# Down-projection weights of a gated FFN: gain and Strassen sums prepared in the up-projections and kept in DRAM, residual rows added to straight from PSUM

## The chip, the cores and the metric

The kernel runs on one core of a Trainium2 chip. The metric is device time in microseconds (us) of one execution; lower is better. A core has TensorE (PE, the matmuls, with PEld for its weight loads), VectorE (DVE), ScalarE (ACT), GpSimd (POOL), and SyncE (SP), whose queue issues nearly all DMAs here. Data lies in DRAM, in SBUF (128 partitions) and in PSUM, where matmuls write.

## The reference

One step of a layer: token mixing with three recurrences, then a gated FFN, then a norm. The change concerns the last product of the FFN and the residual. In the reference `T` is 2048 for the prompt and 4 for each of 8 samples, `D_MODEL` 1024, `D_FF` 2816; all in float32:

```
h = _rmsnorm(x, p['norm_ffn'][l]) * (1 + sc2) + sh2
gate, b_ffn = _causal_dwconv(h @ p['ffn_w_gate'][l], b_ffn, p['ffn_conv_w'][l])
gate = gate + p['ffn_conv_b'][l]
x = x + g2 * ((jax.nn.silu(gate) * (h @ p['ffn_w_up'][l])) @ p['ffn_w_down'][l])
...
y = _rmsnorm(x, final_norm)
```

`g2` is a vector of 1024 gains for a sequence, so for the prompt `g2 * (a @ w)` equals `a @ (w * g2)` with each column of `w` taken times its gain.

## The kernel before

Float32 accuracy comes from splitting: `split` (L1812) makes of a tile a rounded part hi (ACT, L1813) and the rest lo (DVE, L1814), and `s_prod` (L1816) makes each block product of three matmuls, hi·hi, hi·lo and lo·hi (L1822 to L1824). On top of it the FFN's products use the Strassen-Winograd scheme: of a 2x2 arrangement of blocks seven products, 1 to 7, take the place of eight, at the price of sums of blocks. The sums of the stationary side are made by `s_combo` on POOL (L1790 to L1802), four for each set of seven products. The sums of the moving side are made once for many sets. A set of eight plain products stands where the sums of the moving side are not ready.

The up-projections (`ffn_up_s`, here from about 1845 to 2299.5 us) run over sets of products with weights as the stationary side; each product is 24 matmuls of 264 columns. DVE there splits the weights (`w_lo<-w_raw,w_hi`), joins the products' partial sums (L2029, L2030) and applies a causal convolution (L1997); the gated rows go to DRAM as `aT`.

The down-projection (`ffn_down_s`, 2299.5 to 2838.4 us) has its moving side, w_down, in three thirds of 3, 4 and 4 row-blocks (`KH`). Inside a third it runs over 8 sets of 256 tokens: the first set plain (products named C.. when complete), the others by Strassen. A generator, `down_tiles`, prepares the third to come: it starts two sets before the old third ends and goes on into the first sets of the new one, because a tile's room is free only when the old third's last product with that tile is done (`freed`). It loads four quarters of w_down for each row-block, splits them as tiles 1, 2, 3 and B, then loads quarters again, makes 5, 6 and 7 by `t_sums` (one subtraction on POOL, L1807, two on DVE, L1808 and L1809) and 4 by two subtractions on POOL (L2213), and splits those. While it has quarters in hand it also issues the matmuls of the 32 sample tokens (`d_sample`, L2239, `mm_ds`, 176 passes in all).

After a product, `after` joins the results. Products 1, 5 and 6 are copied out of PSUM by ACT (`snap`, L2299, into `d_y`). When the partner is done, DVE adds it from PSUM (L2347), multiplies by the gains g2 (L2348), and one step later POOL adds the residual row x (L2351; in the last set DVE does). Plain products and 4 need one multiplication from PSUM (L2344) and the same POOL addition. The row is then stored, or normed and written out in the last third. Residual rows x are loaded three products ahead into the ring of raw tiles (tag "wr", 8 buffers), which the w_down loads share; partial sums have a ring of their own, "sn", of 8.

The order on each engine is not that of the Python code: a list scheduler arranges the instructions by estimated times, and each engine then runs its list in order. DMAs stand in SP's list and wait there for what they store and for a free buffer.

Of the kernel before, what the change touches and what calls it, by code (L numbers as in the profile page):

```python
# [73 lines left out]
class Kern:  # L74
# [94 lines left out]
    def setup(self):  # L169
# [33 lines left out]
        sc("sdn", [NS, D])  # L203

# [1709 lines left out]
    def ffn_up_s(self, pts, open1, down):  # L1914
# [215 lines left out]
        more, at = more(), [0]  # L2130
        for n, (s, P, U, t, b, first, done) in enumerate(seq):
# [15 lines left out]
        self.flush()  # L2147

# [7 lines left out]
    def down_tiles(self, pts, n, freed):  # L2156


        nc = self.nc
        w = self.i["ffn_w_down"][0].rearrange("(k p) c -> p k c", p=128)  # L2160
        kh, k0 = KH[n], 2 * sum(KH[:n])

        T = self.dT[n] = {P: [None] * kh for P in "1234567B"}

        def load(q, k):
            i, j = int(q[0]) - 1, int(q[1]) - 1
            r = self.w_raw()[:, :512]
            self.ld(r, w[:, k0 + kh * i + k, 512 * j:512 * j + 512])
            return r

        def put_t(P, k, raw):
            tag = P.replace("B", "4")
            p = pts[k // 2](tag)
            T[P][k] = t = (p.tile([128, 2 * NP], F32R, name="t_hi", tag=f"{tag}h{k % 2}")[:, :512],
                           p.tile([128, 2 * NP], F32R, name="t_lo", tag=f"{tag}l{k % 2}")[:, :512])
            self.split(*t, raw)

        raws = {}
        order = [(q, P, k) for q, P in (("11", "1"), ("21", "2"), ("22", "3"), ("12", "B")) for k in range(kh)]
        for x in order[:SWR - 1]:  # L2180
            raws[x] = load(x[0], x[2])
        for m, x in enumerate(order):
            while x[1].replace("B", "4") not in freed:
                yield
            put_t(x[1], x[2], raws.pop(x))
            if m + SWR - 1 < len(order):
                y = order[m + SWR - 1]
                raws[y] = load(y[0], y[2])
            if m % 2:
                yield  # L2190


        while not {"5", "6", "7"} <= freed:
            yield
        q = None
        for k in range(kh + 1):
            old, q = q, None
            if k < kh:
                q = {x: load(x, k) for x in ("12", "11", "22")}
                yield  # L2200
                self.d_sample(k0 + k, (q["11"], q["12"]))
                self.t_sums(q)
            for P in "576" if old else ():
                put_t(P, k - 1, old[P])
                yield
        while "C" not in freed:
            yield
        r = [(load("21", k), load("22", k)) for k in range(2)]
        for k in range(kh):
            yield  # L2210
            self.d_sample(k0 + kh + k, r[k])
            for x in T["6"][k]:
                nc.gpsimd.tensor_tensor(r[k][0], r[k][0], x.bitcast(F32), op=ALU.subtract)  # L2213
            if k:
                put_t("4", k - 1, r[k - 1][0])
            if k + 2 < kh:
                r.append((load("21", k + 2), load("22", k + 2)))
        yield
        put_t("4", kh - 1, r[kh - 1][0])

    def ffn_down_s(self, p, pts, work, freed):
# [9 lines left out]
        g = p.tile([128, D], F32, name="g2")  # L2231
        self.ld(g, self.ap(self.dram["modr"], 5 * D, [[0, 128], [1, D]]))
# [9 lines left out]
        self.d_sample = sample  # L2242
# [30 lines left out]
        outs, xs = {}, {}  # L2273
# [463 lines left out]
```

## Time and profile before

| | us |
|---|---|
| median of 3 runs | 2845.62 (2843.83 to 2852.76) |
| profiled execution | 2848.95 |
| its span in the trace | 2847.2 |

The page's head and its slices of the span:

```profile
span 2847.2 us, 54532 instructions
PE 2715.1 (95%) x19969; PEld 2462.4 (86%) x19969; DVE 1888.8 (66%) x3767; ACT 1267.9 (45%) x2795; POOL 930.2 (33%) x1353
PE   6999999999999999999999999989999989999888
DVE  4535777577676778565565546596776677867777
POOL 3311223311113422111121102254344447565675
```

A slice is 71 us; each digit is the busy share in tenths. The up-projections by Strassen are the slices from about 26 to 32, the down-projection the last eight: there POOL, little used before, is busy for half and more of the time. Busy time of PE is counted from the start of the first to the end of the last of the matmuls that follow one another without a gap, so that a lower clock shows as longer matmuls and not as idle time; the prediction therefore counts matmuls and takes their undisturbed step.

### The profile page before, as it was taken

Reading aid. Unit: us, or ns where it says so; the run is one execution under the profiler, and the core shown is the slowest. Engines: PE = TensorE matmul, PEld = TensorE weight load, DVE = VectorE, ACT = ScalarE, POOL = GpSimd, SP = SyncE. Lnnn points to the kernel's source line nnn. Section 1 sums busy time; section 2 is a strip of 40 time slices with the busy share of each in tenths; the row PEclk is TensorE's granted clock in tenths of the full one; section 3 lists DMA queues with packets and bytes.
Section 4 is the critical chain, followed back from the end, with each engine's and each line's share of the span. In section 5 each row is a group of like instructions: output and inputs, shape, how many; then the busy total and the mean of one; then the engine's idle time right before and its main releaser. Section 6 shows DMA issues by size and latency. Waiting matters only on the chain.

```text
span 2847.2 us, 54532 instructions
## 1 busy us (share of the span) xinstructions
PE 2715.1 (95%) x19969; PEld 2462.4 (86%) x19969; DVE 1888.8 (66%) x3767; ACT 1267.9 (45%) x2795; POOL 930.2 (33%) x1353
## 2 busy tenths in 40 slices
PE   6999999999999999999999999989999989999888
PEld 4999888889989999999999989989999967667566
DVE  4535777577676778565565546596776677867777
ACT  4534445455554545544443323454444443423333
POOL 3311223311113422111121102254344447565675
PEclk8999999999999999999999999999999999999999
DMA  6465436675556697553553345752222266756542
GB/s 234 132 207 151 127 111 175 182 227 144 176 165 196 213 283 198 159 154 114 183 151 105 107 147 153 217 180 80 90 69 79 77 198 188 255 157 194 177 147 96
DMA packets 543106, 455.30 MB, mean 160 GB/s; under 512 B 83302, under 2 KB 475142, under 8 KB 541814
## 3 DMA queue, kind: packets, MB, share of 16 engines
q1 hardware_dynamic: 542838, 451.82, 52.4%
q8 instruction: 157, 2.57, 0.4%
q14 instruction: 111, 0.91, 0.1%
HBM read 310.17 MB, written 141.53 MB: 159 GB/s over the span
## 4 chain that ended last, share of the span: by engine, by line
PE 44%; DVE 6%; POOL 5%; DMA 4%; issue 3%; ACT 1%; SPq 0%; POOLq 0%; DVEq 0%; ACTq 0%
PE mm_f L608 5%; PE mm_f L610 5%; PE mm_f L609 5%; PE s_x L1823 3%; PE s_x L1822 3%; PE s_x L1824 3%; PE d_ps L1822 3%; PE d_ps L1823 3%; PE d_ps L1824 2%; POOL d_y L2351 2%; PE s_y L1822 1%; PE s_y L1823 1%; PE s_y L1824 1%; DVE t_lo L1814 1%; DVE w_lo L1814 1%
## 5 line engine op out<-in xcount | busy, mean ns | idle before, releaser
L608 PE MATMUL mm_f<-g_hi,w_hi 128*128 128x384 f32 (+2 forms) x2016 | 663.0, 329 | 4.0 <-ACT g_hi L579 3.9
L609 PE MATMUL mm_f<-g_lo,w_hi 128*128 128x384 f32 (+2 forms) x2016 | 652.8, 324 | 0.5 <-DVE g_lo L580 0.4
L610 PE MATMUL mm_f<-g_hi,w_lo 128*128 128x384 f32 (+2 forms) x2016 | 652.4, 324 | 0.0
L608 PEld LDWEIGHTS mm_f<-g_hi,w_hi 128*128 128x128 f32 x2016 | 381.9, 189 | 25.9 <-issue 14.8
L609 PEld LDWEIGHTS mm_f<-g_lo,w_hi 128*128 128x128 f32 x2016 | 382.6, 190 | 6.8 <-issue 4.8
L610 PEld LDWEIGHTS mm_f<-g_hi,w_lo 128*128 128x128 f32 x2016 | 382.2, 190 | 6.4 <-issue 5.7
L1822 PE MATMUL d_ps<-t_hi,w_hi 128*128 128x512 f32 x627 | 257.5, 412 | 23.0 <-ACT t_hi L1813 12.8
L1823 PE MATMUL d_ps<-t_lo,w_hi 128*128 128x512 f32 x627 | 256.2, 409 | 13.4 <-DVE t_lo L1814 13.4
L1824 PE MATMUL d_ps<-t_hi,w_lo 128*128 128x512 f32 x627 | 248.0, 405 | 6.3 <-DVE w_lo L1814 6.3
L556 DVE TENSOR_TENSOR w_lo<-w_raw,w_hi 128x512 fp32r<-128x512 f32 (+1 forms) x236 | 163.7, 700 | 75.8 <-ACT w_hi L555 71.6
L555 ACT CAST w_hi<-w_raw 128x512 fp32r<-128x512 f32 (+1 forms) x236 | 144.1, 619 | 137.7 <-PE mm_f L609 96.2
L1822 PE MATMUL s_x<-t_hi,w_hi 128*128 128x264 f32 x704 | 200.7, 285 | 2.5 <-DVE sy L2030 1.4
L1823 PE MATMUL s_x<-t_lo,w_hi 128*128 128x264 f32 x704 | 200.4, 285 | 0.0
L1824 PE MATMUL s_x<-t_hi,w_lo 128*128 128x264 f32 x704 | 199.1, 283 | 0.5 <-DVE w_lo L1814 0.5
L1814 DVE TENSOR_TENSOR w_lo<-a_raw,w_hi 128x512 fp32r<-128x512 f32 (+1 forms) x159 | 154.8, 984 | 52.0 <-ACT w_hi L1813 49.0
L2351 POOL TENSOR_TENSOR d_y<-d_y,t_raw 128x512 f32<-128x512 f32 x92 | 144.8, 1576 | 127.3 <-DVE d_y L2348 53.8
L1813 ACT CAST w_hi<-a_raw 128x512 fp32r<-128x512 f32 (+1 forms) x159 | 91.6, 583 | 208.7 <-PE d_ps L1823 125.8
L1822 PEld LDWEIGHTS d_ps<-t_hi,w_hi 128*128 128x128 f32 x627 | 121.6, 194 | 68.6 <-ACT t_hi L1813 16.7
L1814 DVE TENSOR_TENSOR w_lo<-w_raw,w_hi 128x512 fp32r<-128x512 f32 x156 | 112.9, 726 | 76.7 <-ACT w_hi L1813 75.2
L1823 PEld LDWEIGHTS d_ps<-t_lo,w_hi 128*128 128x128 f32 x627 | 121.5, 194 | 48.5 <-DVE t_lo L1814 19.3
L1813 ACT CAST w_hi<-w_raw 128x512 fp32r<-128x512 f32 x156 | 96.2, 619 | 138.0 <-PE s_x L1823 69.6
L1824 PEld LDWEIGHTS d_ps<-t_hi,w_lo 128*128 128x128 f32 x627 | 121.6, 194 | 36.7 <-DVE w_lo L1814 8.1
(574 smaller groups left out, 6811.1 us busy)
## 6 DMA issues: line engine op xcount, KB each, us to landing
t_raw<-in_ffn_w_down_dram SPq DMA_DIRECT2D x99, 256.0 KB
w_raw<-in_w_in_dram SPq DMA_DIRECT2D x96, 256.0 KB
t_raw<-x SPq DMA_DIRECT2D x96, 256.0 KB
w_raw<-in_ffn_w_gate_dram SPq DMA_DIRECT2D x94, 256.0 KB
w_raw<-in_ffn_w_up_dram SPq DMA_DIRECT2D x94, 256.0 KB
ada_w<-in_w_ada_dram SPq DMA_DIRECT2D x32, 512.0 KB
R<-recB SPq DMA_DIRECT2D x16, 1024.0 KB
x<-d_y SPq DMA_DIRECT2D x64, 256.0 KB
```

Of the source, the lines that this page charges most:

```text
L555: nc.scalar.copy(hi[:, :n], raw[:, :n])
L556: nc.vector.tensor_sub(lo[:, :n], raw[:, :n], hi[:, :n].bitcast(F32))
L608: nc.tensor.matmul(ps[:, :N], wh, hi[:, k, :N], start=(k == 0), stop=False)
L609: nc.tensor.matmul(ps[:, :N], wh, lo[:, k, :N], start=False, stop=False)
L610: nc.tensor.matmul(ps[:, :N], wl, hi[:, k, :N], start=False, stop=(k == 7))
L1813: self.nc.scalar.copy(hi, src)
L1814: self.nc.vector.tensor_sub(lo, src, hi.bitcast(F32))
L1822: self.nc.tensor.matmul(ps, hi[:, k], th, start=(start and k == 0), **f)
L1823: self.nc.tensor.matmul(ps, hi[:, k], tl, start=False, **f)
L1824: self.nc.tensor.matmul(ps, lo[:, k], th, start=False, stop=(k == n - 1), skip_group_check=True)
L2351: (nc.vector if s == len(sets) - 1 else nc.gpsimd).tensor_tensor(y, y, x, op=ALU.add)
```

## The change

1. `down_sums`, new, runs in the up-projections, advanced once a product from step `8 * n_plain + 8` on. For each of the 11 row-blocks it loads the four quarters of w_down (128x512, 256 KB), has DVE multiply each by its gains, stores the results (tiles 1, B, 3, 2) to a new scratch tensor `wdT` in DRAM, has POOL make four subtractions (5, 7, 6, 4), and stores these. That is 44 loads, 44 multiplications, 44 subtractions and 88 stores. The gains g2 are loaded there.
2. `down_tiles` loads finished tiles from `wdT` and splits them, in the order 1, 5, 6, 2, 3, B, 7, 4. The sums of L1807 to L1809 and L2213 are gone, the number of splits is the same.
3. `after` adds products straight from PSUM to the residual row on DVE: products 1, 5 and 6 to the rows 11, 22 and 12, then the partners, or for plain products and 4 the one result. The copies by ACT, the multiplications by gains and the separate additions on POOL are gone. The residual rows are now loaded into the ring "sn", of 10 buffers, three products ahead of the first addition.
4. The sample's matmuls are a generator of their own, `samples`, with 44 loads of w_down, advanced in the list `states` after products 1, 3 and 6 of sets that are not a third's last.

The loads from w_down so go from 99 to 88, and 88 loads from and 88 stores to `wdT` are new.

```diff
+NSN = 10
...
+            if n >= 8 * n_plain + 8:
+                next(sums, None)
...
+    def down_sums(self):
...
+        g = self.pev.tile([128, D], F32, name="g2", tag="g2", bufs=1)
+        self.ld(g, self.ap(self.dram["modr"], 5 * D, [[0, 128], [1, D]]))
...
+                for _ in range(2):
+                    yield
+                for x, P in (("11", "1"), ("12", "B"), ("22", "3"), ("21", "2")):
+                    j = int(x[1]) - 1
+                    nc.vector.tensor_tensor(q[x], q[x], g[:, 512 * j:512 * j + 512], op=ALU.mult)
+                    put(P, x)
+                    if x in ("12", "21"):
+                        yield
+                yield
+                for P, o, a, b in (("5", "11", "12", "11"), ("7", "12", "22", "12"), ("6", "22", "22", "11"),
+                                   ("4", "21", "21", "22")):
+                    nc.gpsimd.tensor_tensor(q[o], q[a], q[b], op=ALU.subtract)
+                    yield
+                    put(P, o)
...
     def down_tiles(self, pts, n, freed):
...
+        order = [(P, k) for P in "15623B74" for k in range(kh)]
...
+            self.ld(r, self.dram["wdT"]["123B567".index(P) if P != "4" else 7, row + k])
...
-                self.t_sums(q)
...
-            for x in T["6"][k]:
-                nc.gpsimd.tensor_tensor(r[k][0], r[k][0], x.bitcast(F32), op=ALU.subtract)
...
-                xs[outs[m]] = x = self.w_raw()[:, :512]
-                self.ld(x, place(*outs[m]))
+                xs[needs[m]] = x = p.tile([128, 512], F32, name="d_y", tag="sn", bufs=NSN)
+                self.ld(x, place(*needs[m]))
...
-            if P in "156":
-                c["s" + P] = snap(c["V" if P == "5" else "X"])
+            add = lambda name, ps: nc.vector.tensor_tensor(xs[s, name], ps, xs[s, name], op=ALU.add)
+            first = {"1": ("11", "X"), "5": ("22", "V"), "6": ("12", "X")}.get(P)
+            if first:
+                add(first[0], c[first[1]])
...
-                nc.vector.tensor_tensor(y, c[{"1": "Y", "3": "V", "7": "X"}[P]], y, op=ALU.add)
-                nc.vector.tensor_tensor(y, y, g[:, cs], op=ALU.mult)
-
-            def rest():
-                (nc.vector if s == len(sets) - 1 else nc.gpsimd).tensor_tensor(y, y, x, op=ALU.add)
...
+            add(name, c[b])
+            y = xs.pop((s, name))
...
-        states = itertools.chain(self.lru_states(p, "so", 1), self.ffn_states(p, "so", 1))
+        states = itertools.chain(samples(), sample_out(), self.lru_states(p, "so", 1), self.ffn_states(p, "so", 1))
...
-            if not plain(s) and q < nq - 1 and P in ("36" if n == len(KH) - 1 else "6"):
+            if not plain(s) and q < nq - 1 and P in "136":
```

How the scheduler places this, in the order of instructions. On DVE in the up-projections, where the sums begin; `w_lo` is the rest part of a weight tile, `su` and `sy` are gate rows, `t_raw` with `g2` are the new multiplications. Before:

```order
L2030 TENSOR_TENSOR sy_22784<-sy_22784,s_y_22954 128x264
L1814 TENSOR_TENSOR t_lo_23079<-t_raw_22769,t_hi_23078 128x528
L1814 TENSOR_TENSOR w_lo_23017<-w_raw_23014,w_hi_23016 128x512
L663 SCALAR_TENSOR_TENSOR sy_22852<-su_22736,sy_22852 128x528
L1814 TENSOR_TENSOR t_lo_23021<-t_raw_22895,t_hi_23020 128x528
L1814 TENSOR_TENSOR t_lo_23083<-t_raw_22897,t_hi_23082 128x528
L2029 TENSOR_TENSOR su_23114<-s_y_23047,sn_23112 128x264
```

Of the changed kernel:

```order
L2032 TENSOR_TENSOR sy_22785<-sy_22785,s_y_22955 128x264
L2176 TENSOR_TENSOR t_raw_23413<-t_raw_23413,g2_23409 128x512
L1816 TENSOR_TENSOR w_lo_23018<-w_raw_23015,w_hi_23017 128x512
L665 SCALAR_TENSOR_TENSOR sy_22853<-su_22737,sy_22853 128x528
L1816 TENSOR_TENSOR t_lo_23022<-t_raw_22896,t_hi_23021 128x528
L2176 TENSOR_TENSOR t_raw_23415<-t_raw_23415,g2_23409 128x512
L2176 TENSOR_TENSOR t_raw_23417<-t_raw_23417,g2_23409 128x512
L1816 TENSOR_TENSOR t_lo_23084<-t_raw_22898,t_hi_23083 128x528
L2031 TENSOR_TENSOR su_23115<-s_y_23048,sn_23113 128x264
L2176 TENSOR_TENSOR t_raw_23746<-t_raw_23746,g2_23409 128x512
L2176 TENSOR_TENSOR t_raw_23748<-t_raw_23748,g2_23409 128x512
```

The multiplications stand between the splits, some of them two in a row. The first of the 44 stands at row 2403 of DVE's list and the last at row 2595; 42 splits of weight products (`w_lo`) lie between them; with POOL's subtractions, shown next, the sums stand beside 46.

On POOL at the same place, where `w_raw` are the sums of `s_combo`. Before:

```order
L1795 TENSOR_TENSOR w_raw_23014<-w_raw_22802,w_raw_22804 128x512
L2005 COPY cv_s_23229<-sffn_1045 128x8x2
L1801 TENSOR_TENSOR w_raw_22802<-w_raw_22800,w_raw_22802 128x512
L2005 COPY cv_s_23354<-sffn_1045 128x8x2
L2116 TENSOR_TENSOR t_raw_22897<-t_raw_22897,t_raw_22895 128x528
L1797 TENSOR_TENSOR w_raw_23014<-w_raw_23014,w_raw_22800 128x512
L1799 TENSOR_TENSOR w_raw_22798<-w_raw_22798,w_raw_23014 128x512
L1994 COPY su_23275<-fhalo_1042 128x2
```

Of the changed kernel:

```order
L2118 TENSOR_TENSOR t_raw_22898<-t_raw_22898,t_raw_22896 128x528
L2183 TENSOR_TENSOR t_raw_23411<-t_raw_23413,t_raw_23411 128x512
L1799 TENSOR_TENSOR w_raw_23015<-w_raw_23015,w_raw_22801 128x512
L2183 TENSOR_TENSOR t_raw_23413<-t_raw_23415,t_raw_23413 128x512
L1801 TENSOR_TENSOR w_raw_22799<-w_raw_22799,w_raw_23015 128x512
L2183 TENSOR_TENSOR t_raw_23415<-t_raw_23415,t_raw_23411 128x512
L2183 TENSOR_TENSOR t_raw_23417<-t_raw_23417,t_raw_23415 128x512
L1996 COPY su_23276<-fhalo_1043 128x2
L2183 TENSOR_TENSOR t_raw_23746<-t_raw_23748,t_raw_23746 128x512
```

The new subtractions (L2183) now stand between the sums of `s_combo`, from row 791 to row 902 of POOL's list.

On DVE at the end of the first third, where the tiles of the second are split (`t_lo`); `w_lo` belongs to the running set, `d_y` are output rows. Before:

```order
L2347 TENSOR_TENSOR d_y_29450<-d_ps_29423,d_y_29450 128x512
L1814 TENSOR_TENSOR t_lo_29596<-t_raw_29514,t_hi_29595 128x512
L2348 TENSOR_TENSOR d_y_29450<-d_y_29450,g2_28372 128x512
L1814 TENSOR_TENSOR w_lo_29487<-a_raw_29484,w_hi_29486 128x384
L2347 TENSOR_TENSOR d_y_29433<-d_ps_29400,d_y_29433 128x512
L2348 TENSOR_TENSOR d_y_29433<-d_y_29433,g2_28372 128x512
L1814 TENSOR_TENSOR t_lo_29559<-t_raw_29508,t_hi_29558 128x512
L1814 TENSOR_TENSOR t_lo_29565<-t_raw_29510,t_hi_29564 128x512
```

Of the changed kernel:

```order
L2334 TENSOR_TENSOR d_y_29600<-d_ps_29635,d_y_29600 128x512
L1816 TENSOR_TENSOR w_lo_29750<-a_raw_29721,w_hi_29749 128x384
L1816 TENSOR_TENSOR t_lo_29801<-t_raw_29753,t_hi_29800 128x512
L2334 TENSOR_TENSOR d_y_29708<-d_ps_29784,d_y_29708 128x512
L1816 TENSOR_TENSOR t_lo_29807<-t_raw_29755,t_hi_29806 128x512
L1816 TENSOR_TENSOR w_lo_29781<-a_raw_29561,w_hi_29780 128x384
L1816 TENSOR_TENSOR t_lo_29829<-t_raw_29757,t_hi_29828 128x512
L1816 TENSOR_TENSOR t_lo_29855<-t_raw_29761,t_hi_29854 128x512
L2334 TENSOR_TENSOR d_y_29735<-d_ps_29812,d_y_29735 128x512
```

The gain steps (L2348) are gone, and the splits of the new tiles stand between the splits of the running set and the additions from PSUM (L2334).

More of the change, by code (lines that the diff above doesn't have):

```diff
@@ L2129, in more @@
                 put_t(1, c, "4", last[c])
-        more, at = more(), [0]
+        more, at, sums = more(), [0], self.down_sums()
         for n, (s, P, U, t, b, first, done) in enumerate(seq):
@@ L2171, in put_t @@
-        def put_t(P, k, raw):
+            self.ld(r, self.dram["wdT"]["123B567".index(P) if P != "4" else 7, row + k])
+            raws.append(r)
+        for x in order[:SWR - 1]:
+            load(*x)
+        for m, (P, k) in enumerate(order):
+            while ("C" if P == "4" else P.replace("B", "4")) not in freed:
+                yield
             tag = P.replace("B", "4")
             p = pts[k // 2](tag)
-            T[P][k] = t = (p.tile([128, 2 * NP], F32R, name="t_hi", tag=f"{tag}h{k % 2}")[:, :512],
-                           p.tile([128, 2 * NP], F32R, name="t_lo", tag=f"{tag}l{k % 2}")[:, :512])
-            self.split(*t, raw)
@@ L2178, in down_tiles @@
[L2178 to L2185, printed above, removed]
+            t = (p.tile([128, 2 * NP], F32R, name="t_hi", tag=f"{tag}h{k % 2}")[:, :512],
+                 p.tile([128, 2 * NP], F32R, name="t_lo", tag=f"{tag}l{k % 2}")[:, :512])
@@ L2186, in down_tiles @@
+            self.split(*t, raws.pop(0))
+            T[P][k] = t
             if m + SWR - 1 < len(order):
-                y = order[m + SWR - 1]
-                raws[y] = load(y[0], y[2])
+                load(*order[m + SWR - 1])
             if m % 2:
                 yield
[L2193 to L2201, printed above, removed]
-                self.t_sums(q)
-            for P in "576" if old else ():
-                put_t(P, k - 1, old[P])
-                yield
@@ L2241, in sample, with samples @@
                                  start=(len(done) == 1), stop=(len(done) == NFB), tile_position=(0, 32 * j))
-        self.d_sample = sample
+        def samples():
+            w = self.i["ffn_w_down"][0].rearrange("(k p) c -> p k c", p=128)
+            r = []
+            for k in range(NFB + 1):
+                if k < NFB:
+                    r.append([self.w_raw()[:, :512] for _ in range(2)])
+                    for h in range(2):
+                        self.ld(r[k][h], w[:, k, 512 * h:512 * h + 512])
+                    yield
+                if k:
+                    sample(k - 1, r[k - 1])
         nq = SEQ // 256
@@ L2272, in ffn_down_s @@
         count = dict(X=0, V=0)
[L2273 removed]
+        needs, xs = {}, {}
         for m, (s, P, U, t, b, begins, ends) in enumerate(seq):
[L2275 to L2276 removed]
+            name = ends[1:] if plain(s) and ends else None if plain(s) else {"1": "11", "5": "22", "6": "12", "4": "21"}.get(P)
+            if name:
+                needs[m] = s, name
         def place(s, name):
@@ L2368, in sample_out @@
                 cs = slice(512 * h, 512 * h + 512)
-                y, gs, x = sn(), self.w_raw()[:, :512], self.w_raw()[:, :512]
+                y, gs, x = (self.w_raw()[:, :512] for _ in range(3))
                 self.ld(y[:NS], d[:, cs])
```

79 lines of the change are left out of this document (30 added, 49 removed).

## The prediction

> **What bounds the kernel now.** I read the page's slices first (PE at 99% or 100% nearly throughout, lower only at the end), then the table by windows over the two stages that the change touches, then the same table for the matmuls of the down-projection alone, then the groups by line, and last the timeline of the places where PE stands.
>
> Windows of all instructions; the columns are window, length, busy time and count of PE, PEld, DVE, ACT, POOL, the granted clock, the DMA share and GB/s:
>
> ```profile
> 1900.00:2000.00 100.00, 100.00 (x826) 100.00 (x825) 70.48 (x123) 47.87 (x93) 44.92 (x60) 1.00 0.26 80
> 2200.00:2300.00 100.00, 100.00 (x824) 99.91 (x823) 76.71 (x137) 52.43 (x103) 38.52 (x44) 1.00 0.32 97
> 2320.00:2360.00 40.00, 29.33 (x125) 17.75 (x124) 33.13 (x39) 14.89 (x28) 29.05 (x20) 0.87 0.61 190
> 2380.00:2430.00 50.00, 48.39 (x211) 38.27 (x210) 37.95 (x49) 17.44 (x34) 34.60 (x27) 1.00 0.64 189
> 2640.00:2715.00 75.00, 61.55 (x259) 40.56 (x258) 57.08 (x61) 25.69 (x49) 50.00 (x38) 0.89 0.51 161
> ```
>
> In the up-projections (to 2299.5 us) PE never stands: 100 us hold 826 matmuls, 0.121 us each, so a product of 24 takes 2.91 us and a set of seven 20.3 us. There every microsecond by which another engine falls behind is new time, and the spare room of DVE and POOL is a quarter and a half. In the down-projection PE loses time in three places, where a third of w_down is exchanged (2320, 2460 and 2640), with DVE busy 76 to 83% and the clock down to 0.87.
>
> Windows of the d_ps matmuls alone (PE, PEld, DVE, ACT), then two matmuls 11 steps apart in a stretch without a gap, and a group of the sample's passes:
>
> ```profile
> 2299.50:2320.00 20.50, 19.57 (x84) 15.59 (x85) 1.89 (x3) 0.00 (x0) 1.00 0.75 226
> 2320.00:2360.00 40.00, 25.85 (x87) 16.20 (x86) 3.68 (x6) 2.81 (x5) 0.87 0.61 190
> 2360.00:2460.00 100.00, 96.08 (x406) 75.32 (x405) 16.85 (x25) 8.82 (x16) 1.00 0.77 238
> 2460.00:2525.00 65.00, 49.44 (x173) 33.88 (x172) 5.46 (x8) 2.80 (x5) 0.87 0.58 186
> 2525.00:2640.00 115.00, 113.17 (x482) 89.74 (x481) 15.60 (x23) 8.80 (x16) 1.00 0.62 185
> 2640.00:2715.00 75.00, 55.60 (x195) 38.78 (x194) 6.26 (x10) 2.80 (x5) 0.89 0.51 161
> 2715.00:2838.40 123.40, 113.77 (x462) 88.50 (x461) 14.99 (x22) 8.77 (x16) 0.96 0.38 122
> ...
> 2299.49 0.40 PE L1822 MATMUL d_ps<-t_hi,w_hi 128*128 128x512 f32 x1
> 2302.05 0.39 PE L1824 MATMUL d_ps<-t_hi,w_lo 128*128 128x512 f32 x1
> ...
> 2314.19 1.07 PE L2239 MATMUL mm_ds<-t_raw,d_sam 128*32 128x256 f32 x16
> ```
>
> The step is (2302.05 - 2299.49) / 11 = 0.232 us, and a sample pass 1.07 / 16 = 0.067 us. What a window is longer than its matmuls at that step is its loss. 2320 to 2360 holds 87 d_ps and 32 sample passes: 40 - 20.2 - 2.1 = **17.7 us**. 2460 to 2525 (64 sample passes, 4.3 us): 65 - 40.1 - 4.3 = **20.6**. 2640 to 2715 (64): 75 - 45.2 - 4.3 = **25.5**. The steady windows lose 5.8, 3.2 and 16.2, together **25.2**. The stage so holds 89 us that are not matmul, and this is all that the change can win.
>
> **The change, part by part: the down-projection.** What stands before the matmuls in an exchange (start, length, group; in brackets the idle time and its end; then groups by line over the stage: busy, mean ns, idle before):
>
> ```profile
> 2324.51 0.50 PE L1823 MATMUL d_ps<-t_lo,w_hi 128*128 128x512 f32 x1 [2.06 <-DVE t_lo L1814]
> 2328.81 0.80 PE L1823 MATMUL d_ps<-t_lo,w_hi 128*128 128x512 f32 x1 [3.34 <-DVE t_lo L1814]
> 2329.41 0.63 PE L1824 MATMUL d_ps<-t_hi,w_lo 128*128 128x512 f32 x1
> ...
> L1814 DVE TENSOR_TENSOR t_lo<-t_raw,t_hi 128x512 fp32r<-128x512 f32 x79 | 74.1, 954 | 11.1 <-ACT t_hi L1813 10.5
> L1807 POOL TENSOR_TENSOR t_raw<-t_raw 128x512 f32<-128x512 f32 x11 | 17.9, 1631 | 10.3 <-PE mm_ds L2239 10.2
> L1808 DVE TENSOR_TENSOR t_raw<-t_raw 128x512 f32<-128x512 f32 x11 | 12.6, 1147 | 4.8 <-POOL t_raw L1807 4.8
> L2213 POOL TENSOR_TENSOR t_raw<-t_raw,t_hi 128x512 f32<-128x512 f32 x11 | 17.1, 1557 | 17.3 <-PE mm_ds L2239 17.2
> L2347 DVE TENSOR_TENSOR d_y<-d_ps,d_y 128x512 f32<-128x512 f32 x63 | 43.1, 684 | 22.7 <-PE d_ps L1824 20.9 <-issue 1.7
> L2348 DVE TENSOR_TENSOR d_y<-d_y,g 128x512 f32<-128x512 f32 x63 | 60.2, 955 | 0.9
> L2351 POOL TENSOR_TENSOR d_y<-d_y,t_raw 128x512 f32<-128x512 f32 x92 | 144.8, 1576 | 127.3 <-DVE d_y L2348 53.8
> L2299 ACT COPY d_y<-d_ps 128x512 f32<-128x512 f32 x63 | 34.8, 581 | 0.0
> ```
>
> PE waits for t_lo, the last step of a chain: load, sample matmul, POOL sum, two DVE sums, ACT cast, DVE subtraction; after a gap of 3.34 us the next matmuls start 0.60 us apart, the half-rate tail. The change cuts the three sums and the sample's place out of the chain; load, cast and subtraction stay, as many as before. In an exchange DVE now has, for four row-blocks, 4 x 8 = 32 splits, of which some 24 stand in the last set, 11 w_lo, 8 adds from PSUM, and POOL's 4 s_combo. By 0.68 for a split (L1814's median below) and L2347's 0.684: 24 x 0.68 + 11 x 0.68 + 8 x 0.684 = 29.3, and 4 held turns of about 1.2 (below): **34 us**. Over it PE has six products of the old third's last set and four of the new third's first: (72 + 48) x 0.232 = 27.8 us to the last third, (54 + 48) x 0.232 = 23.7 to the second, whose old row-blocks are three. DVE so stays behind by 34 - 27.8 = 6 in the exchange to the last third, and I take its loss as 6 in place of 25.5: **-19**. To the second it is ten behind: 20.6 to 10, **-10**. The start has the same splits but its tiles wait for loads that share queue SP with the x rows and the sample's tensor, at a DMA share of 0.75: 17.7 to 10, **-8**. Bounds of the three together: -64 (all goes) and 0 (the splits alone set it).
>
> Steady windows: 63 mults of L2348 (60.2 us), 92 adds of POOL (144.8 us) and 63 copies of ACT go; 63 adds of about 0.68 come to DVE. DVE is left about even, POOL is relieved by more than half, and the stretch of DVE by POOL (t_lo's mean of 954 against 683 for the same shape, below) lessens. But the first product's bank is now freed by DVE, where ACT with 17.44 of 50 us freed it; and a row is now held from its load over both adds to its store, ten buffers against eight for the partial sums and eight for the rows before. I take **-11** of 25.2, bounds -25 and +20: the upper is one wait of 0.8 us for a bank or row in each of the 24 sets. The 176 sample passes keep their 12 us, spread over quiet sets: 0.
>
> Tail (start, length, group):
>
> ```profile
> 2838.46 0.69 DVE L2344 TENSOR_TENSOR d_y<-d_ps,g 128x512 f32<-128x512 f32 x1 [0.98 <-PE d_ps L1824]
> 2839.19 0.69 DVE L2351 TENSOR_TENSOR d_y<-d_y,t_raw 128x512 f32<-128x512 f32 x1
> ```
>
> After the last matmul two DVE steps become one: **-1** (0.73).
>
> **The up-projections: what the sums cost.** 44 mults on DVE, 44 subtractions on POOL, 44 loads and 88 stores come in. By the instruction order they stand not over all the sets from step 40, but packed within 46 products: 46 x 24 x 0.121 = 134 us. How DVE and POOL get on (start, length, group; then a tile's shortest, median and longest ns, then groups by line over 1900 to 2280):
>
> ```profile
> 2383.13 1.30 POOL L2351 TENSOR_TENSOR d_y<-d_y,t_raw 128x512 f32<-128x512 f32 x1
> 2383.35 1.64 DVE L2348 TENSOR_TENSOR d_y<-d_y,g 128x512 f32<-128x512 f32 x1
> ...
> 2389.65 1.54 POOL L2351 TENSOR_TENSOR d_y<-d_y,t_raw 128x512 f32<-128x512 f32 x1 [2.22 <-DVE d_y L2344]
> 2389.95 0.68 DVE L2347 TENSOR_TENSOR d_y<-d_ps,d_y 128x512 f32<-128x512 f32 x1
> ...
> L1814 DVE TENSOR_TENSOR w_lo<-w_raw,w_hi x132: 672/683/1601, 1899.7 to 2279.6; 128x512 fp32r<-128x512 f32 x132
> L1797 POOL TENSOR_TENSOR w_raw<-w_raw x19: 1277/1288/1782, 1913.2 to 2276.0; 128x512 f32<-128x512 f32 x19
> ...
> L1797 POOL TENSOR_TENSOR w_raw<-w_raw 128x512 f32<-128x512 f32 x19 | 28.8, 1515 | 30.4 <-DVE w_lo L1814 30.4
> L1997 DVE SCALAR_TENSOR_TENSOR sy<-su,par,sy 128x528 f32<-128x528 f32 x38 | 41.3, 1087 | 10.9 <-ACT sy L1995 10.9
> ```
>
> A DVE instruction with both inputs in SBUF, begun at 2383.35 beside POOL's, ends at 2384.99, 0.56 after POOL's end at 2384.43; the one that reads PSUM takes its usual 0.68 beside POOL. So the two take turns at something of SBUF: POOL holds it for 1.15 to 1.29 us an instruction, DVE for 0.55 to 0.68. The sums ask 44 x (1.15 + 0.55) = 75 to 44 x (1.29 + 0.68) = 87 us of turns. What is free: the windows of 1900 and 2200 have DVE at 70 to 77 us and POOL at 39 to 45 of 100; without DVE's PSUM reads and what lies over one another, the turns fill about three quarters (between 68 and 86% by the shortest and the full lengths), so 19 to 43 of 134 us are free, 33 at three quarters. Lower demand less that, less some 4 us of finished products ahead of PE: 75 - 33 - 4 = **+38**, which falls on PE at 100%. Bounds: 0, where the split of the coming products stays ahead and the sums, which nobody waits for before 2299, take only the gaps; and +63 = 87 - 24 with no lead. The order speaks against the lower end: sums stand in line ahead of w_lo and of s_combo, and an in-order engine does not pass them. The stores wait in SP's one line for DVE and POOL, ahead of the loads of up-projection weights; 132 transfers are room enough at a DMA share of 0.26 to 0.32, so I price this line at nothing of its own.
>
> The Trainium skill, "SBUF — State Buffer", section "Who interferes with whom", speaks against the change: it says that a VectorE instruction with two SBUF inputs and a GpSimd instruction reading SBUF shut each other out for the whole instruction, and that one with at most one SBUF input is not hindered. The rows at 2383 and 2389 agree; by the rule without any overlap the term is the upper bound, +63.
>
> **Sum**, against the profiled execution's 2848.95 us (span 2847.2): +38 - 8 - 10 - 19 - 11 - 1 = **-11**, so 2838. That execution lies 3.3 us above the median of 2845.62, so for a median **2835 us**.
>
> **Rivals.** First, the sums hide in the up-projections: 49 us of gain remain, 2797. For it: PE has no gap there at all, and DVE 23 to 30% idle; against it: the packing and the turns. Second, slower: DVE and POOL take whole turns in the packed stretch, +63 - 49 = +14, **2860**; it turns slower as soon as that stage gives up more than 49 us, and by a measurable amount past 58. For it: L1797's mean of 1515 beside its shortest of 1277 already now. Third, the exchanges gain only half (-18) and the steady windows nothing, since DVE's splits, not the sums, set their pace: +38 - 19 = +19, 2865. For it: t_lo of L1814 ends both gaps quoted; against it: the 10 to 17 us that POOL stood behind mm_ds in that chain. That the sums are not used in time cannot be: the first is wanted after 2299 and the last made before.
>
> **How the numbers follow.** About 0.3%, 8.5 us, is what a measurement can tell here: faster is below 2837, slower above 2854. Forecast 0.50 (faster 0.29, within 0.21: it lies near the edge), first rival 0.22 (faster), second 0.16 (slower 0.12, within 0.04), third 0.12 (slower 0.09, within 0.03). So faster 0.51, within 0.28, slower 0.21. The range 2793 to 2864 takes in the first two rivals and leaves out about 0.1 above and 0.08 below; the forecast's own is 2820 to 2850.
>
> **What would show it.** Right: the d_ps stage some 49 us shorter, its first matmul some 38 us later, PE with gaps behind w_lo or w_hi in the stretch of the gain mults, L1814 there well over 734 ns. Wrong: PE at 100% through the sums (first rival); gaps in the exchanges still ended by t_lo with more than 35 us lost in the three (third); a wait for d_y's rows ahead of begin matmuls in steady sets, which I priced within the bound only.

## The result, and the profile after

| | before | changed |
|---|---|---|
| median (lowest to highest), us | 2847.42 (2843.83 to 2852.76), 4 runs | 2831.69 (2829.4 to 2834.18), 4 runs |
| profiled execution, us | 2848.95 | 2829.4 |
| first s_x to first d_ps (the up-projections), us | 463.7 | 500.6 |
| first to last d_ps (the down-projection), us | 538.5 | 484.3 |

The ratio to before is 0.9943, 95% interval 0.9924 to 0.9962: 0.6% faster, 15.7 us between the medians. Of the 19.6 us between the profiled executions the down-projection gives 54.2, the up-projections take 36.9 back, and 2.3 come from stages ahead of both.

Both lengths are read from the first and last starts of a tile's instructions, here of the changed kernel (count: shortest, median, longest ns, first and last start). Line numbers have moved: L1824 to L1826 are the three matmuls, L1815 and L1816 the split.

```profile
L1824 PE MATMUL s_x<-t_hi,w_hi x704: 281/284/589, 1833.5 to 2339.7; 128*128 128x264 f32 x176
L1824 PE MATMUL d_ps<-t_hi,w_hi x627: 387/392/628, 2334.1 to 2818.0; 128*128 128x512 f32 x157
L1826 PE MATMUL d_ps<-t_hi,w_lo x627: 387/394/628, 2336.5 to 2818.5; 128*128 128x512 f32 x157
```

The last s_x matmul starts after the first d_ps matmul: one product of the up-projections, 24 matmuls or 2.9 us of PE, now stands inside the down-projection. It does so in every run below but e6. Against before, the up-projections thus cost 36.9 + 2.9 = 39.8 us and the down-projection saves 54.2 + 2.9 = 57.1; between runs that both have it nothing changes.

The windows of all instructions of the changed kernel, over the stretch of the sums and the rest of the up-projections (columns as in the prediction):

```profile
1888.00:2059.00 171.00, 140.53 (x1055) 136.40 (x1056) 166.04 (x207) 55.06 (x112) 140.68 (x113) 0.94 0.78 262
2060.00:2330.00 270.00, 270.00 (x2226) 270.00 (x2225) 193.79 (x340) 132.23 (x259) 115.96 (x148) 1.00 0.29 88
```

The sums fill 171 us in which DVE is busy for 166 and POOL for 141, and PE does in them what takes 128 us undisturbed (1055 x 0.121): the 43 us that are missing are about what the stage grew by. In the 270 us that follow PE has no gap and DVE is idle for 76 of them, POOL for 154: the room was there, but later. The timeline of one stall (DVE, then POOL, then PE):

```profile
1926.61 1.77 DVE L1999 SCALAR_TENSOR_TENSOR sy<-su,par,sy 128x528 f32<-128x528 f32 x1
1928.31 1.76 DVE L665 SCALAR_TENSOR_TENSOR sy<-su,sy 128x528 f32<-128x528 f32 x1
1930.00 1.75 DVE L2176 TENSOR_TENSOR t_raw<-t_raw,g 128x512 f32<-128x512 f32 x1
1931.67 1.75 DVE L1816 TENSOR_TENSOR w_lo<-w_raw,w_hi 128x512 fp32r<-128x512 f32 x1
...
1926.10 8.45 POOL L2183 TENSOR_TENSOR t_raw<-t_raw 128x512 f32<-128x512 f32 x5
...
1933.47 0.59 PE L1826 MATMUL s_x<-t_hi,w_lo 128*128 128x264 f32 x1 [5.28 <-DVE w_lo L1816]
```

Five subtractions stand in a row on POOL, 1.69 us each. Beside them every DVE instruction takes 1.75 us, one for one, where the same shapes take 0.68 to 0.80 undisturbed. PE stood 5.28 us for the w_lo that came fourth in that line.

The windows of d_ps in the changed kernel (PE, PEld, DVE; ACT has nothing left here), then of the sample's passes:

```profile
2334.00:2355.00 21.00, 18.29 (x77) 14.30 (x78) 0.00 (x0) 1.00 0.92 275
2355.00:2395.00 40.00, 32.93 (x132) 23.51 (x130) 11.53 (x17) 1.00 1.03 347
2395.00:2475.00 80.00, 66.55 (x258) 46.24 (x258) 20.01 (x29) 1.00 0.71 221
2475.00:2520.00 45.00, 42.59 (x183) 33.71 (x181) 8.87 (x13) 1.00 1.04 360
2520.00:2640.00 120.00, 116.27 (x494) 92.05 (x494) 28.20 (x41) 1.00 0.59 184
2640.00:2690.00 50.00, 47.84 (x198) 37.78 (x197) 8.80 (x13) 0.97 0.70 232
2690.00:2818.60 128.60, 127.58 (x548) 102.05 (x546) 30.71 (x45) 1.00 0.42 132
...
2355.00:2395.00 40.00, 6.91 (x56) 2.05 (x56) 0.00 (x0) 1.00 1.03 347
2395.00:2475.00 80.00, 17.23 (x88) 4.05 (x88) 0.00 (x0) 1.00 0.71 221
2520.00:2640.00 120.00, 3.16 (x32) 1.17 (x32) 0.37 (x1) 1.00 0.59 184
```

At 0.232 us a matmul and 0.067 a pass, the start of the stage (2355 to 2395) loses 40 - 30.6 - 3.8 = 5.6 us, the exchange at 2475 loses 45 - 42.5 = 2.5 and the one at 2640 loses 50 - 45.9 = 4.1. The clock in these windows is 0.97 to 1.00, where it was 0.87 to 0.89. The largest loss now lies in a quiet window, 2395 to 2475: 80 - 59.9 - 5.9 = 14.2 us, with 88 sample passes in 26 places in it and no gap on PE. The first window, 2334 to 2355, loses nothing: beside its 77 d_ps matmuls it holds 27 others, the late product among them.

### The profile page after: what moved, and what is told of

Read it like the earlier page. It is cut to its first block, busy times and chain, and to the rows that moved or that the text cites. A ratio compares the mean times of both kernels' runs of the same rounds, so it can differ in the third digit from the quotient of the medians.

```text
span 2827.7 us, 54627 instructions
## 1 busy us (share of the span) xinstructions
PE 2709.6 (96%) x19969; PEld 2461.6 (87%) x19969; DVE 1848.7 (65%) x3785; ACT 1235.5 (44%) x2732; POOL 804.9 (28%) x1272
## 4 chain that ended last, share of the span: by engine, by line
PE 73%; DMA 10%; DVE 8%; issue 3%; ACT 3%; POOL 2%; SPq 1%; DVEq 0%; POOLq 0%; ACTq 0%
PE mm_f L610 10%; PE mm_f L612 10%; PE mm_f L611 10%; PE d_ps L1824 5%; PE d_ps L1826 5%; PE d_ps L1825 5%; PE s_x L1824 2%; PE s_x L1825 2%; PE s_x L1826 2%; PE mm_t L653 2%; PE mm_t L654 1%; PE mm_t L656 1%; DMA w_raw<-oT 1%; DVE w_lo L1816 1%; PE ssq L729 1%
## 5 line engine op out<-in xcount | busy, mean ns | idle before, releaser
L610 PEld LDWEIGHTS mm_f<-g_hi,w_hi 128*128 128x128 f32 x2016 | 381.5, 189 | 25.9 <-issue 14.6
L1824 PE MATMUL d_ps<-t_hi,w_hi 128*128 128x512 f32 x627 | 250.0, 400 | 5.6 <-ACT w_hi L1815 3.6
L1825 PE MATMUL d_ps<-t_lo,w_hi 128*128 128x512 f32 x627 | 247.3, 395 | 0.0
L1826 PE MATMUL d_ps<-t_hi,w_lo 128*128 128x512 f32 x627 | 243.5, 398 | 0.6 <-DVE w_lo L1816 0.6
L1824 PE MATMUL s_x<-t_hi,w_hi 128*128 128x264 f32 x704 | 204.1, 290 | 20.1 <-ACT sn L1985 8.6
L1826 PE MATMUL s_x<-t_hi,w_lo 128*128 128x264 f32 x704 | 201.7, 288 | 11.3 <-DVE w_lo L1816 11.2
L1815 ACT CAST w_hi<-a_raw 128x512 fp32r<-128x512 f32 (+1 forms) x159 | 92.8, 584 | 266.2 <-PE d_ps L1825 200.2
L2334 DVE TENSOR_TENSOR d_y<-d_ps,d_y 128x512 f32<-128x512 f32 x159 | 108.8, 687 | 139.0 <-PE d_ps L1826 134.0
L1816 DVE TENSOR_TENSOR w_lo<-w_raw,w_hi 128x512 fp32r<-128x512 f32 x156 | 126.5, 813 | 56.0 <-ACT w_hi L1815 55.3
L1815 ACT CAST w_hi<-w_raw 128x512 fp32r<-128x512 f32 x156 | 96.3, 619 | 147.4 <-PE s_x L1825 50.4
L1824 PEld LDWEIGHTS d_ps<-t_hi,w_hi 128*128 128x128 f32 x627 | 118.1, 188 | 45.3 <-ACT w_hi L1815 11.0
L1824 PEld LDWEIGHTS s_x<-t_hi,w_hi 128*128 128x128 f32 x704 | 134.5, 191 | 23.5 <-ACT sn L1985 9.8
L683 DVE SCALAR_TENSOR_TENSOR qy<-cv_u,par,qy 128x384 f32<-128x384 f32 (+1 forms) x216 | 122.8, 571 | 38.9 <-POOL cv_u L674 23.5
L1826 PEld LDWEIGHTS d_ps<-t_hi,w_lo 128*128 128x128 f32 x627 | 118.1, 188 | 31.6 <-DVE d_y L2334 2.9
```

What stands on the lines that cost most here:

```text
L610: nc.tensor.matmul(ps[:, :N], wh, hi[:, k, :N], start=(k == 0), stop=False)
L683: nc.vector.scalar_tensor_tensor(y[:, :n], u[:, j:j + n], cw[:, j, blk:blk + 1], y[:, :n], op0=ALU.mult, op1=ALU.add)
L1815: self.nc.scalar.copy(hi, src)
L1816: self.nc.vector.tensor_sub(lo, src, hi.bitcast(F32))
L1824: self.nc.tensor.matmul(ps, hi[:, k], th, start=(start and k == 0), **f)
L1825: self.nc.tensor.matmul(ps, hi[:, k], tl, start=False, **f)
```

## The experiments

All lengths are from one profile each. Totals with a ratio are medians of four to six runs, and the ratio is to runs of before taken beside them; the other totals are of the one profiled execution. "Up" is first s_x to first d_ps, "down" first to last d_ps.

| run | up, us | down, us | total, us |
|---|---|---|---|
| before | 463.7 | 538.5 | 2848.95 |
| changed | 500.6 | 484.3 | 2829.4 |
| e1 transfers alone | 460.9 | 483.4 | 2779.66 |
| e2 subtractions on DVE | 485.2 | 485.7 | 2808.76 |
| e3 paced | 491.8 | 486.2 | 2823.62, ratio 0.9901 (0.9886 to 0.9915) |
| e4 paced, on DVE | 477.6 | 482.0 | 2809.25, ratio 0.9862 (0.9842 to 0.9882) |
| e5 snapshots back | 500.8 | 483.9 | 2819.17 |
| e6 sums back | 474.7 | 498.9 | 2818.28 |
| e7 finely paced, on DVE | 502.1 | 484.1 | 2829.33, ratio 0.9938 (0.9919 to 0.9956) |
| e8 passes together | 500.2 | 479.8 | 2824.38 |
| e9 old finish in full | 501.2 | 500.4 | 2849.3 |
| e10 tied multiplications | 465.1 | 481.0 | 2795.43, ratio 0.9812 (0.9793 to 0.983) |
| e11 the same, passes together | 464.9 | 480.0 | 2785.42, ratio 0.9777 (0.9753 to 0.9801) |
| e12 best version | 465.3 | 478.9 | 2790.05, ratio 0.9788 (0.9769 to 0.9806) |

How far such a length can be trusted shows where the code of a stage is the same: down is that of the changed kernel in e1 to e4, e7 and e10, and comes out from 481.0 to 486.2 us; up is the same in changed, e5, e8 and e9, from 500.2 to 501.2.

**Transfers alone (e1).** Multiplications and subtractions are left out; stores keep their places, so the down-projection multiplies by raw quarters and its result is not the layer's:

```diff
-                    nc.vector.tensor_tensor(q[x], q[x], g[:, 512 * j:512 * j + 512], op=ALU.mult)
...
-                    nc.gpsimd.tensor_tensor(q[o], q[a], q[b], op=ALU.subtract)
```

> The 44 multiplications and 44 subtractions of the sums are left out; the 44 loads and 88 stores stay, and the stores write the raw quarters, so the down-projection works with other numbers and its output is not the layer's. Watched is the stretch from the first s_x matmul of the up-projections to the first d_ps: 463.7 us before, 500.6 in the changed kernel. Theory A (DVE and POOL take turns, and the sums overfill these turns): the stretch falls to 464 to 470. Theory B (the 132 new transfers in SP's one line or on the DMA engines delay the weight loads): it stays at 490 or more. The down-projection should keep its length of 484 us from first to last d_ps under both.

Up took 460.9 us, with the late product 463.8, as before. The window of that run over the transfers, all instructions:

```profile
1880.00:2060.00 180.00, 179.53 (x1464) 179.32 (x1465) 127.10 (x221) 81.77 (x159) 77.44 (x98) 0.99 0.81 278
```

PE is busy for 179.53 of 180 us at a DMA share of 0.81: the 132 transfers and SP's line cost nothing that can be seen. Here the stores wait for loads alone and not for the sums; but in the changed kernel too, between 1880 and 2300 us, the only wait for a load of up-projection weights that the trace shows is one of 0.5 us. Theory B falls, and what is lost is lost on DVE and POOL.

**Subtractions on DVE (e2).**

```diff
-                    nc.gpsimd.tensor_tensor(q[o], q[a], q[b], op=ALU.subtract)
+                    nc.vector.tensor_tensor(q[o], q[a], q[b], op=ALU.subtract)
```

> The 44 subtractions go from POOL to DVE, all else as in the changed kernel. Theory A: 88 DVE instructions ask 88 x 0.68 = 60 us of turns where the mixed pairs asked 75 to 87, against 33 free in the packed stretch: the loss of 37 us falls to 20 to 27, the stretch to 484 to 491. Theory B: stores wait in SP's line as before and DVE finishes them no sooner: 498 or more. A third view, that DVE's own time is the limit and POOL does not matter: DVE has more to do, 505 or more.

Up took 485.2, inside theory A's 484 to 491: the loss fell from 36.9 to 21.5 although DVE has 44 instructions more. So 15.4 us of the loss are the price of having POOL do the subtractions. The 21.5 that stay are DVE's own: 88 more instructions, packed into 158 us (1881.7 to 2040.1).

**Paced sums (e3, e4).** A one-column copy ties each load to the running product; e4 also has the subtractions on DVE:

```diff
                     q[x] = r = self.w_raw()[:, :512]
+                    nc.scalar.copy(r[:, :1], self.now[0][:, 0, :1].bitcast(F32))
                     self.ld(r, w[:, k0 + kh * i + k, 512 * j:512 * j + 512])
```

> A one-column copy on ACT from the weight tile of the running product into each raw quarter, ahead of its load, ties the loads of the sums to the products; the sums then stand beside 92 splits and not 42. The work of DVE, POOL and SP on them is the same. Theory A: 92 x 2.91 = 268 us with a quarter free gives 67 against a demand of 75 to 87, less 4 of lead: the loss falls from 37 to 4 to 16, the stretch to 468 to 480, and the whole kernel to some 2800 to 2812 in a measurement where the changed kernel has 2832. Theory B: the same stores wait in the same line, 495 or more.

> Pacing and subtractions on DVE together. Theory A: a demand of 60 against 67 free: the loss is 0 to 6, the stretch 464 to 470, the whole kernel 2795 to 2802. If POOL's turns do not matter and DVE's own time does: DVE, 70% busy in the up-projections, goes to 70 + 60/268 = 92%, and the loss is not smaller than with pacing alone.

Both missed: 491.8 where 468 to 480 was expected, and 477.6 where 464 to 470 was. The difference between the two, 14.2 us, is again POOL's part, as between the changed kernel and e2 (15.4). But 14 to 28 us stay. Spreading was expected to remove them, so bursts within a row-block or DVE's mean load were suspected next.

**Finely paced (e7).** Each quarter is tied and loaded by itself, with load, multiplication and subtraction a product apart:

```diff
+                    nc.scalar.copy(r[:, :1], self.now[0][:, 0, :1].bitcast(F32))
+                    self.ld(r, w[:, k0 + kh * i + k, 512 * j:512 * j + 512])
+                    yield
+                    nc.vector.tensor_tensor(r, r, g[:, 512 * j:512 * j + 512], op=ALU.mult)
+                    put(P, x)
+                    yield
+                    for P, o, a, b in sums.get(x, ()):
+                        nc.vector.tensor_tensor(q[o], q[a], q[b], op=ALU.subtract)
+                        put(P, o)
```

> Subtractions on DVE as in the second run, and each raw quarter tied on its own to the running product by the copy on ACT, so that a multiplication and one or two subtractions stand at every second product in place of a whole row-block at once. Theory A as it stands after four runs (the sums cost where they come in bursts that DVE cannot take between two sets): the loss of the up-projections falls from 14 us to 0 to 6, the stretch to 464 to 470, the whole kernel to 2794 to 2804. If a burst is not the cause but the mean load of DVE at 90%: 474 to 480 again.

It was the worst of all: 502.1. What DVE waits for in the up-projections (total us, times, longest) points to a cause, first in e7:

```profile
DVE t_raw L2176 <- DMA t_raw<-in_ffn_w_down_dram: 44.6, 22, 4.2
DVE t_raw L2180 <- DMA wdT<-t_raw: 14.1, 10, 3.9
```

and in e4:

```profile
DVE t_raw L2177 <- DMA t_raw<-in_ffn_w_down_dram: 19.8, 14, 5.2
DVE t_raw L2184 <- DMA wdT<-t_raw: 3.0, 3, 2.1
```

The tie puts the load right ahead of its multiplication, and the in-place subtraction overwrites what a store still reads. The multiplication then stands at the head of DVE's list until the load lands, and the splits, partial sums and convolutions of the up-projections behind it stand too. In the changed kernel that wait was 0.5 us in all. So the pacing had brought a wait of its own. In e3 DVE stood 16.1 us for these loads and POOL 15.9 us for these stores.

**Tied multiplications (e10).** As finely spread as e7, on DVE. Loads run a row-block ahead and are not tied; the multiplication is, through one column of the gains that ACT writes anew; sums go to tiles of their own, so that they wait for no store:

```diff
+                nc.scalar.activation(h[:, :1], self.now[0][:, 0, :1].bitcast(F32), AF.Identity, scale=0.0,
+                                     bias=gc[:, j:j + 1])
+                nc.vector.tensor_tensor(r, r, h, op=ALU.mult)
...
+                    t = self.w_raw()[:, :512]
+                    nc.vector.tensor_tensor(t, q[a], q[b], op=ALU.subtract)
```

> Subtractions on DVE; the quarters are loaded a row-block ahead without a tie; each multiplication is tied to the running product by an ACT step that rewrites one column of the gains (old value plus zero times a weight column); sums go to raw tiles of their own, so that they wait for no store. In the finely tied run DVE stood 44.6 us for loads and 14.1 us for stores at its head of line, against 0.5 in the changed kernel, and the up-projections lost 38 us. Theory A with that cause: these waits fall under 10 us together, the loss to 0 to 8, the stretch to 464 to 472, the whole kernel 2794 to 2806. If the mean load of DVE, some 90%, is the cause: 478 or more.

Up took 465.1, 1.4 us more than before the change, 4.3 with the late product. DVE's whole wait for a load of the sums is one line:

```profile
DVE t_raw L2184 <- DMA t_raw<-in_ffn_w_down_dram: 1.7, 1, 1.7
```

The same 88 instructions on DVE thus cost 21.5 us packed (e2), 38 spread with waits (e7) and 1.4 spread without, each 2.9 more with the late product. DVE's mean load is so ruled out, and in e7 the waits were the cause. In e3 and e4, where a row-block's work also comes at once, the share of the bursts was not measured. In e10 and in e11 below, tiles 6 and 4 are formed from other operands (22 less 11, 21 less 22), the same count and size; the down-projection works with these other numbers, and its result is not the layer's.

**Snapshots back (e5).** Ready tiles stay; for products 1, 5 and 6 and their partners `after` copies by ACT and adds the residual by POOL as before, without gains. Plain products and 4 keep the direct addition, and residual rows come into the ring of raw tiles again:

```diff
-                add(first[0], c[first[1]])
+                c["s" + P] = snap(c["V" if P == "5" else "X"])
...
+            nc.vector.tensor_tensor(y, c[b], x if one else y, op=ALU.add)
+            def rest():
+                if not one:
+                    (nc.vector if s == len(sets) - 1 else nc.gpsimd).tensor_tensor(y, y, x, op=ALU.add)
```

> Ready tiles from DRAM stay, the direct additions go: products 1, 5 and 6 are copied by ACT again, POOL adds the residual row of those outputs again (63 additions, 63 copies), and residual rows come into the ring of raw tiles, of 8. Only the gain multiplications stay out. Watched is the time from first to last d_ps: 538.5 us before, 484.3 in the changed kernel. Theory C (the direct additions carry a part, because POOL's additions held DVE up and lay ahead of s_combo): 490 to 505. Theory D (the ready tiles carry all): 484 to 487. The up-projections stay at about 500 under both.

Down took 483.9, as theory D has it to 0.1. POOL's 60 additions of 1.49 us and ACT's 63 copies are back, and the total does not show it:

```profile
L2359 POOL TENSOR_TENSOR d_y<-d_y,t_raw 128x512 f32<-128x512 f32 x60 | 89.5, 1492 | 138.7 <-DVE d_y L2354 122.3 <-DMA t_raw<-in_ffn_w_down_dram 11.6 <-DMA a_raw<-aT 4.9
```

The total hides something, though. The last 652 d_ps matmuls, from the exchange to the last third on, have no sample pass among them. They take 159.4 us here and 154.0 in the changed kernel (154.0 to 154.4 in the nine other runs with ready tiles and direct additions), so in the last third the direct additions are worth some 5 us. What made up for it lies ahead: each edit moves the scheduler's order, and the sample's passes stand in 33 places here and in 39 in the changed kernel.

**Old finish in full (e9).** The run before, plus the multiplications, here by a tile of ones:

```diff
+            if one:
+                nc.vector.tensor_tensor(y, c[b], one_, op=ALU.mult)
+            else:
+                nc.vector.tensor_tensor(y, c[b], y, op=ALU.add)
+                nc.vector.tensor_tensor(y, y, one_, op=ALU.mult)
```

> The finish of before in full (copies by ACT, 63 additions and 96 multiplications on DVE, 92 additions on POOL), with ready tiles: since these have their gains already, the multiplications are by a tile of ones, at the same cost as by gains. It is the run with snapshots plus the multiplications. From first to last d_ps that run took 483.9 us, before took 538.5. Theory G (DVE's 60 us of gain multiplications with both inputs in SBUF were what held the steady sets): 495 to 510. Theory D (ready tiles carry all): 483 to 488.

Down took 500.4: theory G. The groups by line show what came back (busy, mean ns, idle before):

```profile
L2364 POOL TENSOR_TENSOR d_y<-d_y,t_raw 128x512 f32<-128x512 f32 x92 | 138.9, 1512 | 153.6 <-DVE d_y L2357 81.1 <-DVE d_y L2360 56.8 <-DMA t_raw<-in_ffn_w_down_dram 5.9
L2360 DVE TENSOR_TENSOR d_y<-d_y,ones 128x512 f32<-128x512 f32 x63 | 55.1, 875 | 0.9
```

The 63 multiplications, with the 32 more additions on POOL that they entail for plain products and 4, cost 16.5 us (500.4 less 483.9), 10.4 of them in the last 652 d_ps matmuls (169.8 less 159.4). The multiplications were not run without those additions.

**Sums back (e6).** The changed kernel's finish, with the sums made in the exchanges from quarters that have their gains; the tiles also come in the order of before, 1, 2, 3, B, then 5, 7, 6 and 4:

```diff
+                q = {x: load(x, k) for x in ("12", "11", "22")}
+                yield
+                self.t_sums(q)
...
+            for x in T["6"][k]:
+                nc.gpsimd.tensor_tensor(r[k][0], r[k][0], x.bitcast(F32), op=ALU.subtract)
```

> Direct additions stay; the four differences of each row-block are made in the exchanges again, from quarters that already have their gains (one subtraction on POOL and two on DVE, then two on POOL for tile 4, as before the change, but without the sample passes in the chain). The up-projections keep 44 multiplications, 44 loads and 44 stores. Theory D or C with a large part for the tiles: the time from first to last d_ps rises from 484 to 505 to 530. If the splits alone set the pace of the exchanges: 484 to 490. Up-projections by theory A: 44 x 0.68 = 30 us against 33 free, a stretch of 464 to 470 in place of 500.6.

Down took 498.9, 14.6 more and under the range; up 474.7, over its range. There the 44 multiplications were packed in 93 us (1888.1 to 1981.4): a quarter of that is 23 us, and not the 33 that the expectation had taken from the longer stretch, against a demand of 30. Making the sums in the up-projections as the change does cost 25.9 us (500.6 less 474.7) and saved 14.6. With the late product, which e6 does not have, these are 28.8 and 17.5; the order of the tiles, and 30 places for the sample's passes in place of 39, are in the second figure.

**Passes together (e8).**

```diff
+                if k % 3 == 2 or k == NFB - 1:
+                    for b in range(k, k - k % 3 - 1, -1):
+                        sample(b, r[b])
...
-            for j in range(4):
+            for j in (3, 2, 1, 0):
```

> The sample's passes are issued for three row-blocks at a time, and the last quarter loaded is used first, so that a group waits as a whole; in the order of instructions the passes then stand in 27 places among the d_ps matmuls and not 39. In the changed kernel the steps into and out of such a place take 0.32 and 0.35 us against 0.23 and 0.06 for steps inside: some 0.4 us a place. If that is a price of each place: 484.3 less 12 x 0.4, 479 to 480 from first to last d_ps. If the passes' time is a matter of their number: 484 as before.

Down took 479.8, as expected at 0.4 us for each of 12 places. That it fits so well is partly luck: the steps into, inside and out of the places take 9.6 us less in all, 2.8 of it for 12 steps that now lie between d_ps matmuls, and longer waits in the exchange to the second third give some 2 back.

**Both (e11), and the best version (e12).** e12 is e11 with tiles 6 and 4 formed rightly.

> The run before it, and the sample's passes by three row-blocks. If both gains stand by themselves: up-projections as in that run, 479 to 480 us from first to last d_ps, some 4 to 5 us less in all: 2789 to 2802. If one gives back the other, no less than the run before it.

Up 464.9, down 480.0: down gained 1.0 beside e10 and not 4 to 5. The steps at the places take 9.8 us less again, 2.8 of it for the 12 new steps, but PE waits 5.9 us longer between d_ps matmuls, mostly in the exchange to the second third. Also, e10's 481.0 is the lowest of the seven profiles with passes in 39 places, whose mean is 483.8; e8, e11 and e12, with 27, have 479.8, 480.0 and 478.9. The median total stands 10 us lower than e10's and under the range; in the profiled executions 7.5 of 8.7 us come ahead of the change, where the first s_x begins at 1830.5 and not at 1838.0.

> As the run before (each multiplication tied to its product, loads a row-block ahead, sums in tiles of their own, the sample's passes by three row-blocks), with tile 6 formed from 22 and tile 5, and tile 4 from 21 and tile 6, where the two runs before took 22 less 11 and 21 less 22: the same count and size of instructions, two of them now wait for the sum before them on the same engine. Theory A: 463 to 468 us in the up-projections, 479 to 482 from first to last d_ps, 2781 to 2793 in all. If the chain of the two sums brings waits back: the stretch at 470 or more.

Up 465.3 and the total as expected, down 478.9, just under its range. Its window over the sums, to be set against the one of 1888 to 2059 above:

```profile
1918.00:2200.00 282.00, 279.83 (x2294) 278.81 (x2294) 253.15 (x428) 132.26 (x289) 143.92 (x147) 1.00 0.59 197
```

DVE is busy for 90% over 282 us and PE stands idle for 2 of them. At a ratio of 0.9788 (0.9769 to 0.9806) to before, against 0.9943 (0.9924 to 0.9962), it is faster than both kernels.

## Why the prediction was right, point by point

It forecast 2835 us, 11 less than before; 2831.7 was measured, 15.7 less by the medians. The up-projections came out as priced, and by the mechanism it named. The down-projection gave 57.1 us (with the late product) where the terms add up to 49: the exchanges gave 14.6 more than priced, the steady windows 5 less and the tail 1 less. That these partly cancel is luck, and so are the 2.3 us from stages ahead of the change.

- **Up-projections, +38: measured +36.9, with the late product +39.8.** The cause was shown: without the work on DVE and POOL no loss (e1), without POOL's share of the sums 15.4 us less (e2, as the count of turns forecast), and with the work on DVE, spread over 280 us without waits, 1.4 (e10). No run has POOL's subtractions spread without waits. The stretch was longer than I had it, 171 us and not 134, as PE itself was slowed in it. The second rival's +63 did not come (nor does its 24 us of free turns follow from the working, which has 19 to 43), and the first, sums that hide, fails for this order of instructions, but it is what e10 and e12 are. The Trainium skill, "SBUF — State Buffer", section "Who interferes with whom", says that a VectorE instruction with two SBUF inputs and a GpSimd one that reads SBUF shut each other out; the timeline above agrees that they do (1.75 us beside POOL, 0.68 alone), but not without any overlap, as the rival's 63 has it. A pair takes 1.69 us there, where the two alone take 0.68 and 1.28, together 1.96; the term's lower price of 1.15 + 0.55 a pair was the right one.
- **Start and exchanges, -8, -10 and -19: measured -12.1, -18.1 and -21.4** (17.7 to 5.6, 20.6 to 2.5, 25.5 to 4.1). The direction held; the residue was priced too high. I had DVE's splits behind by 6 to 10 us. With POOL's sums and additions gone, t_lo takes 743 ns in place of 954 (839 with POOL's 60 additions back, in e5), as a group of the changed kernel shows:

```profile
L1816 DVE TENSOR_TENSOR t_lo<-t_raw,t_hi 128x512 fp32r<-128x512 f32 x77 | 55.3, 743 | 16.2 <-ACT t_hi L1815 16.2
```

- **Steady windows, -11: measured about -6** (25.2 to 14.2 + 3.3 + 1.5 = 19.0), with a mixed account behind it. The term put together the gain multiplications, POOL's relief and the direct additions. The direct additions are worth nothing in the total by themselves (e5, 483.9 against 484.3) and some 5 us in the last third, and the wait for residual rows that I feared is small: DVE stood 4.6 us for them in all. What was worth 16.5 us, over the whole stage, was the gains that went out with the weights, together with the 32 additions on POOL that hang on them (e9). The additions of the changed kernel, by line:

```profile
L2334 DVE TENSOR_TENSOR d_y<-d_ps,d_y 128x512 f32<-128x512 f32 x159 | 108.8, 687 | 139.0 <-PE d_ps L1826 134.0 <-DMA d_y<-x 4.6
```

- **The sample's passes, 0: this step failed.** The term counted the passes' own 12 us and no price for entering and leaving them. They now stand between d_ps matmuls in 39 places, before in 25. A place costs about 0.4 us: 26 places make some 10 of the 14.2 us in the quiet window, and the 14 that are new some 6 us against before. e8 took 12 places away and gained 4.5.
- **Tail, -1: measured 0.** The span ends 9.2 us after the last d_ps in both.

The gain of 54.2 in the down-projection is thus 16.5 for the multiplications with their additions (e9, beside e5) and 14.6 for the sums (e6), each taken back alone. The other 23 were not taken apart: the sample's passes in the chain of the exchanges, the order of the tiles, the direct additions in the last third and the effect of several of these at once on DVE and POOL are left, and no run tells them from one another.

## What to carry to other kernels

Work moved from a stage where PE waits into one where PE is at 100% is nearly free only where the order of instructions really spreads it (4.3 us here, with all of the sums on DVE, against 39.8): the code advanced the sums over some 290 us (99 products of 2.91), the scheduler's order put them into 171, and DVE and POOL had no room there while they idled afterwards. To spread it, tie the computing instruction to the running work and let its loads go ahead; a tie on the load moves the transfer's latency to the head of an in-order engine (44.6 us of waiting in e7). And an elementwise gain on outputs is cheaper folded into weights that are read once than applied 63 times, while how the outputs are added up was worth little here.

## What the runs showed that I had not expected

- POOL and DVE alternate one instruction at a time where both have work in line: with five subtractions in a row on POOL at 1.69 us, four DVE instructions of 0.68 to 0.80 us took 1.75 to 1.77 each.
- Short matmuls between long ones have a price for each place: in the changed kernel the 39 steps from a d_ps matmul to a sample pass take 0.32 us on average and the 39 back 0.35, against 0.23 for a step between d_ps matmuls and 0.07 for a pass.
- A stage that no kernel here changed moves: the first s_x matmul begins anywhere from 1824.6 (e5) to 1838.0 us (e10). These 13 us are nearly what the change won in all, so single total times were read by their stages.
